# A convolution with max pooling: another load order, another first step, and six column maxima taken in one operation

## The chip, the cores and the metric

The kernel runs on one core of a Trainium2 chip. Its engines work side by side and each takes its own instructions in order: TensorE (PE) multiplies matrices into PSUM, VectorE (DVE) and ScalarE (ACT) work on SBUF and PSUM, GpSimd (POOL) works on SBUF only, and SyncE (SP) issues DMA transfers. An instruction that needs another engine's result waits for it on a semaphore, and everything behind it on the same engine waits too. The metric is the device time of one execution in microseconds (us).

## What is computed

The reference pads each image by one pixel, applies a 3x3 convolution from 64 to 128 channels, and takes the maximum of each 2x2 block. There are 16 images of 64x64.

```python
batch, c_in, h, w, c_out, k = 16, 64, 64, 64, 128, 3
for b, co, ci, kh, kw:   # five loops
    conv[b, co] += weight[co, ci, kh, kw] * x_pad[b, ci, kh:kh+h, kw:kw+w]
output[b, c, i, j] = max(conv[b, c, 2*i:2*i+2, 2*j:2*j+2])
```

## The kernel before

**Tiling.** Two images form a pair: 2 x 64 channels fill 128 partitions, and image l (0 or 1) of a pair uses one half of TensorE's rows. Matmuls of the two halves run at the same time. The 64 rows of an image are cut into four quarters, which gives 8 pairs x 4 quarters = 32 steps. A step makes 8 output rows for each of its two images. SEQ (L10) names the steps: number 0 is K00, 1 is W10, 2 is K01, 3 to 5 are W11, W12 and W13, 6 and 7 are K02 and K03, then the pairs 2 to 7 follow in order. The first digit is the pair, the second the quarter.

**Arithmetic.** Two neighbouring convolution rows have most of their input in common, so the kernel forms sums and differences of input rows and of weights ahead of the products. Each product is three matmuls (kw = 1, 0, 2) of 504 or 512 columns, for one half of one step, and all go through `taps` (L372, matmul at L380). There are two kinds of steps:

- W steps, with four products a half. They need rows prepared: E (difference of even and odd row), S (their sum) and V (differences of rows two apart; for both rows at once, or as two halves Ve and Vo). P2 uses E, P0 and P3 use V, P1 uses S.
- K steps (pair 0), with five products a half. PAa, PAb, PBa and PBb use the input rows as they are, and PR uses KS, a sum of two rows.

Each half step has two PSUM banks, A and B. In a W step P2 goes to A and a copy of A seeds B (SE, ScalarE, L409, once on VectorE as SEv, L407); P0 then adds to A and P3 to B. In a K step PAa and PAb go to A, PBa and PBb to B. In both kinds ScalarE copies A to SBUF (EV, L395 or L397); VectorE takes the row maximum MX of bank B and that copy, back into bank B (L413); and the last product, P1 or PR, adds to B what both rows have in common. That last product therefore waits for MX. Then ScalarE copies the odd columns of B to SBUF (OD, L417), VectorE takes the maximum CM of the even columns and that copy (L423), and a DMA stores the result (ST, L436).

**Weights.** One load (LW) brings all weights. Seven blocks of sums are formed from them as bf16 (`c.` tokens, L215 or L220; GS is an intermediate sum that GM and GP need), turned by TensorE (T, three transposes, L253) and brought to SBUF (TV, L264 or L268). Block D0 serves PBa, D2 PAa, G0 PAb and P0, G2 PBb and P3, G1 PR, GM P2 and GP P1.

**Loads.** Pair 1 (WIDE, L14) stays in fp32 in `wide_x` and is loaded by SP (L278). The first two quarters of pair 0 are loaded as fp32 into `kf` (L283; quarter 0 in the parts a and b) and turned to bf16 in `narrow_x`, odd rows by XO and even rows by XE (L215 or L216). Everything else is loaded by POOL's queue with a cast (LH, L288). The first of these waits for the last XO or XE ahead of it in the order.

**The order.** ORDER (L16) is a list written out, one token for one operation, and the loop at L446 emits the tokens in that order. `MX.5.1` is the row maximum of step 5, half 1; a product's token stands for its next matmul. The letter behind a colon is the engine (v VectorE, a ScalarE, g POOL), a number the PSUM bank. Every engine keeps its own tokens in the order of the list. A row operation on POOL is also held behind the last row operation or cast on VectorE ahead of it in the list (`row_op`, L219).

Of the kernel before, what the change touches and what calls it, by code (L numbers as in the profile page):

```python
# [21 lines left out]
PAa.0.1b PAa.0.0a PAa.0.1b PAa.0.0b PAa.0.1b EV.1.1 PAa.0.0b PAb.0.1b PAa.0.0b PAb.0.1b PAb.0.0a PAb.0.1b
LH.1 PAb.0.0a E.3:v PBa.0.1a:0 TV.G1:a PAb.0.0a PBa.0.0b PBa.0.1a PBa.0.0b PBa.0.1a PBa.0.0b PBa.0.1b EV.0.1
PAb.0.0b PBa.0.1b LH.2 PAb.0.0b PBa.0.1b V.3:v PAb.0.0b P2.3.1:1 PBb.0.0a PBb.0.0a P2.3.1 EV.0.0 PBb.0.0a
LH.3 P2.3.0:4 P2.3.1 P2.3.0 PBb.0.1a PBb.0.1a P2.3.0 SE.3.1:7 PBb.0.1a LH.4 PBb.0.1b KS.0:v PBb.0.0b
PBb.0.1b PBb.0.0b PBb.0.1b PBb.0.0b MX.1.1 P1.1.0 SE.3.0:2 S.3:g P0.3.1 P1.1.0 P0.3.1 P1.1.0 XO.2:a MX.0.0
P0.3.1 P0.3.0 P3.3.1 P0.3.0 P3.3.1 EV.3.1 P0.3.0 MX.0.1 P3.3.1 P3.3.0 P1.1.1 P3.3.0 EV.3.0 E.5:g P1.1.1
P3.3.0 MX.3.1 P1.1.1 PR.0.0 OD.1.0 PR.0.1 PR.0.0 OD.1.1 PR.0.1 MX.3.0 PR.0.0 PR.0.1 XE.2:a PAa.2.0:4 P1.3.1
PAa.2.0 S.5:g CM.1.1 P1.3.1 PAa.2.0 OD.0.1 P1.3.1 P1.3.0 CM.1.0 OD.0.0 PAa.2.1:1 P1.3.0 PAa.2.1 CM.0.1
OD.3.1 P1.3.0 ST.1 PAa.2.1 PAb.2.0 CM.0.0 PAb.2.1 Ve.5:g OD.3.0 PAb.2.0 PAb.2.1 CM.3.1 PAb.2.0 ST.0 PAb.2.1  # L30
PAa.6.0:3 CM.3.0 P2.5.1:0 PAa.6.0 EV.2.1 P2.5.1 KS.6:v PAa.6.0 ST.3 P2.5.1 PAb.6.0 LH.5 PBa.2.1:2 PAb.6.0
KS.2:v PBa.2.1 PAb.6.0 PBa.2.1 PBa.6.0:7 KS.7:v PBb.2.1 EV.6.0 PBa.6.0 PBb.2.1 E.4:v PBa.6.0 PBb.2.1 PBb.6.0
SE.5.1:1 PAa.7.1:5 PBb.6.0 PAa.7.1 MX.2.1 PBb.6.0 Vo.5:g EV.2.0 PAa.7.1 P2.5.0:3 PAb.7.1 P2.5.0 MX.6.0
PAb.7.1 P2.5.0 PAb.7.1 PAa.7.0:4 P0.5.1 SE.5.0:6 PAa.7.0 P0.5.1 LH.6 PAa.7.0 E.9:v P0.5.1 PAb.7.0 EV.7.1
PR.2.1 PAb.7.0 S.8:v PR.2.1 PAb.7.0 EV.5.1 V.9:v PR.2.1 P0.5.0 PBa.7.1:5 P0.5.0 PBa.7.1 EV.7.0 P0.5.0 V.8:v
PBa.7.1 P3.5.0 P3.5.1 EV.5.0 P3.5.0 P3.5.1 P3.5.0 S.9:v P3.5.1 PBa.7.0:0 OD.2.1 P2.9.1:4 E.8:v PBa.7.0
P2.9.1 PBa.7.0 MX.5.1 P2.9.1 V.4:g PBb.7.0 PBb.7.1 PBb.7.0 SE.9.1:3 PBb.7.1 MX.5.0 PBb.7.0 PBb.7.1 PR.6.0
PR.6.0 P0.9.1 PR.6.0 MX.7.0 P0.9.1 P1.5.0 P0.9.1 OD.6.0 P1.5.0 MX.7.1 P1.5.1 P1.5.0 EV.9.1 P1.5.1 PR.7.0
P1.5.1 PR.7.0 S.11:v P3.9.1 PR.7.0 OD.5.0 P3.9.1 P2.9.0:4 CM.6.0 P3.9.1 E.11:g OD.7.0 P2.9.0 CM.5.0 PR.7.1
P2.9.0 OD.5.1 PR.7.1 PBa.2.0:7 CM.7.0 PR.7.1 PBa.2.0 MX.9.1 P2.8.1:6 PBa.2.0 SE.9.0:0 P2.8.1 PBb.2.0 S.4:g  # L40
P2.8.1 PBb.2.0 CM.2.1 OD.7.1 PBb.2.0 P1.9.1 P0.9.0 CM.5.1 P1.9.1 P0.9.0 P1.9.1 CM.7.1 ST.5 P0.9.0 PAa.6.1:1
S.13:g P2.4.0:2 MX.2.0 OD.9.1 PAa.6.1 ST.7 P2.4.0 PAa.6.1 SE.8.1:5 P2.4.0 PAb.6.1 CM.9.1 P3.9.0 PAb.6.1
EV.9.0 P3.9.0 PAb.6.1 Ve.10:v P3.9.0 P0.8.1 SE.4.0:3 PR.2.0 V.13:v P0.8.1 PR.2.0 P0.8.1 PR.2.0 PBa.6.1:4
E.13:v P0.4.0 EV.8.1 PBa.6.1 P0.4.0 PBa.6.1 E.10:v P0.4.0 PBb.6.1 OD.2.0 MX.9.0 P2.8.0:6 PBb.6.1 EV.6.1
V.11:g P2.8.0 PBb.6.1 P2.8.0 P3.8.1 CM.2.0 EV.4.0 P3.8.1 P1.9.0 MX.6.1 P3.8.1 P1.9.0 ST.2 SE.8.0:1 P2.11.1:7
P1.9.0 P2.11.1 P3.4.0 MX.8.1 P2.11.1 OD.9.0 P3.4.0 PR.6.1 P3.4.0 SE.11.1:2 PR.6.1 P0.8.0 CM.9.0 PR.6.1
E.12:g P0.8.0 P1.8.1 MX.4.0 P0.8.0 ST.9 OD.6.1 P1.8.1 P2.13.0:0 P1.8.1 P2.13.0 EV.8.0 CM.6.1 P0.11.1 P2.13.0
P0.11.1 P1.4.0 LH.7 V.12:v OD.8.1 ST.6 P0.11.1 P1.4.0 SE.13.0:6 P2.13.1:4 P1.4.0 P2.13.1 V.14:v P3.8.0
EV.11.1 P2.13.1 P3.8.0 P3.11.1 P3.8.0 CM.8.1 P3.11.1 P0.13.0 OD.4.0 Vo.10:g P3.11.1 P0.13.0 SE.13.1:7 MX.8.0
P2.4.1:5 P0.13.0 P2.4.1 P3.13.0 P2.4.1 EV.13.0 P3.13.0 CM.4.0 P0.13.1 P3.13.0 E.14:v P0.13.1 P1.8.0 SE.4.1:3  # L50
P0.13.1 P1.8.0 MX.13.0 S.10:g P3.13.1 P1.8.0 EV.13.1 P3.13.1 P2.10.0:0 P3.13.1 P2.10.0 MX.11.1 P0.4.1
P2.10.0 OD.8.0 P0.4.1 P1.13.0 P0.4.1 SE.10.0:4 CM.8.0 S.12:g P1.13.0 P1.11.1 P1.13.0 MX.13.1 ST.8 P1.11.1
P2.11.0:1 P1.11.1 OD.13.0 P2.11.0 P3.4.1 P2.11.0 EV.4.1 V.15:v P3.4.1 P0.10.0 P3.4.1 P0.10.0 OD.11.1 P1.13.1
P0.10.0 CM.13.0 SE.11.0:5 P1.13.1 P3.10.0 V.16:g P1.13.1 MX.4.1 P3.10.0 P2.14.1:6 EV.10.0 P3.10.0 P2.14.1
P0.11.0 CM.11.1 P2.14.1 P0.11.0 OD.13.1 P1.4.1 P0.11.0 MX.10.0 SE.14.1:0 P1.4.1 P2.12.0:2 P1.4.1 P2.12.0
CM.13.1 P2.12.0 EV.11.0 P0.14.1 P1.10.0 E.19:v P0.14.1 ST.13 P1.10.0 SE.12.0:7 P0.14.1 P1.10.0 E.18:v
# [469 lines left out]
```

## Time and profile before

| | |
|---|---|
| runs | 101.34, 102.58 and 103.45 us; median 102.58 |
| profiled execution | 101.35 us, span 99.6 us |
| TensorE busy | 93.1 us, 845 matmuls |
| VectorE busy | 91.0 us, 195 operations |
| ScalarE busy | 87.0 us |
| POOL busy | 61.3 us |
| granted TensorE clock | 0.986 on the mean |

The span runs from the first to the last instruction; the execution's own time is 1.75 us longer. Busy time is the time in which at least one instruction of the engine has an open record. Records of neighbouring instructions overlap, since an engine starts one while the end of the one before is still under way, so a row of 0.69 us can stand for 0.60 us of the engine's time. A row of a group ends with the idle time ahead of its instructions and who ended most of it; rows of the timeline begin with start and length in us.

### The profile page before, as it was taken

To read this page: it belongs to the slowest core of one execution; us is meant where nothing else is said; L and a number is where in the kernel's file an instruction comes from. 1 tells how busy PE (TensorE), PEld (TensorE's weight loads), DVE (VectorE), ACT (ScalarE), POOL (GpSimd) and SP (SyncE) were. 2 spreads that over 40 slices of the span, in tenths; PEclk is the share of its full clock that TensorE was granted. 3 is DMA by queue.
4 is the path that set the end of the run, shared out by engine and by line. 5 is a ranking of instruction groups with operands and counts; after the bars stand their busy time and mean duration, and the time that the engine had idled before them with its cause. 6 is when DMAs were issued, how large, how long until landed. Compare 5 with 4: busy or idle time off the path is not lost.

```text
span 99.6 us, 2418 instructions
## 1 busy us (share of the span) xinstructions
PE 93.1 (94%) x845; PEld 61.3 (62%) x845; DVE 91.0 (91%) x195; ACT 87.0 (87%) x196; POOL 61.3 (62%) x58
## 2 busy tenths in 40 slices
...
GB/s 62 286 318 380 336 184 213 213 226 228 246 216 227 226 212 360 230 207 374 148 163 53 109 151 178 205 349 177 16 198 109 105 105 7 100 212 89 73 191 75
DMA packets 11356, 18.81 MB, mean 189 GB/s; under 512 B 848, under 2 KB 9168, under 8 KB 10832
## 3 DMA queue, kind: packets, MB, share of 16 engines
...
q10 hardware_dynamic: 288, 0.20, 0.6%
q8 instruction: 6, 0.10, 0.4%
q14 instruction: 6, 0.05, 0.1%
HBM read 17.07 MB, written 8.39 MB: 256 GB/s over the span
## 4 chain that ended last, share of the span: by engine, by line
PE 87%; DMA 5%; DVE 3%; issue 0%; SPq 0%; DVEq 0%
PE acc L380 86%; DMA wide_x<-in_x_dram 5%; DVE o L423 2%; DVE we L220 1%; PE acc L253 1%; DVE acc L413 0%; SPq L459 0%; DVEq L521 0%
## 5 line engine op out<-in xcount | busy, mean ns | idle before, releaser
L380 PEld LDWEIGHTS <-wt 64*128 64x128 bf16 x816 | 59.0, 94 | 28.9 <-issue 4.0
L380 PE MATMUL acc<-wv,wt 64*128 64x504 bf16 (+1 forms) x240 | 51.8, 377 | 0.0
L380 PE MATMUL acc<-we,wt 64*128 64x512 bf16 (+1 forms) x168 | 42.4, 376 | 0.9 <-DVE we L220 0.9
L413 DVE TENSOR_TENSOR acc<-acc,ev 128x512 f32<-128x512 f32 x64 | 42.4, 689 | 0.7 <-ACT ev L395 0.2
L380 PE MATMUL acc<-ws,wt 64*128 64x512 bf16 (+1 forms) x168 | 40.7, 376 | 0.0
L395 ACT ACTIVATE ev<-acc 128x512 f32<-128x512 f32 x56 | 34.2, 617 | 0.7 <-PE acc L380 0.4
L409 ACT COPY acc<-acc 128x512 f32<-128x512 f32 x55 | 32.9, 601 | 2.0 <-PE acc L380 1.2
L417 ACT COPY od<-acc 128x256 f32<-128x256 f32 x64 | 23.6, 385 | 2.1 <-PE acc L380 1.6
L423 DVE TENSOR_TENSOR o<-acc,od 128x256 f32<-128x256 f32 (+1 forms) x65 | 24.8, 410 | 0.4
L380 PE MATMUL acc<-vh,wt 64*128 64x504 bf16 (+1 forms) x96 | 21.3, 376 | 0.0
L220 POOL TENSOR_TENSOR wv<-narrow_x 128x1024 bf16<-128x1024 bf16 x7 | 14.9, 2130 | 5.3 <-DVE we L220 1.7
L380 PE MATMUL acc<-narrow_x,wt 64*128 64x504 bf16 (+7 forms) x120 | 17.4, 331 | 0.0
L220 POOL TENSOR_TENSOR ws<-narrow_x 128x512 bf16<-128x512 bf16 x12 | 13.7, 1153 | 5.4 <-DVE we L220 2.8
L220 POOL TENSOR_TENSOR we<-narrow_x 128x512 bf16<-128x512 bf16 x9 | 10.3, 1154 | 4.2 <-PE acc L380 1.5
L288 POOL DMA_DIRECT2D narrow_x<-in_x_dram x9 | 5.1, 576 | 8.0 <-ACT narrow_x L215 8.0
L220 POOL TENSOR_TENSOR vh<-narrow_x 128x512 bf16<-128x512 bf16 x5 | 5.8, 1152 | 4.7 <-DVE wv L220 2.1
L220 DVE TENSOR_TENSOR wv<-narrow_x 128x1024 bf16<-128x1024 bf16 x11 | 7.5, 694 | 0.0
L220 DVE TENSOR_TENSOR we<-narrow_x 128x512 bf16<-128x512 bf16 x15 | 6.2, 431 | 0.0
L380 PE MATMUL acc<-ks,wt 64*128 64x504 bf16 (+1 forms) x24 | 5.8, 377 | 0.0
L397 ACT COPY ev<-acc 128x512 f32<-128x512 f32 x8 | 4.8, 596 | 1.0 <-PE acc L380 1.0
L220 DVE TENSOR_TENSOR ws<-narrow_x 128x512 bf16<-128x512 bf16 x12 | 4.9, 412 | 0.0
L441 PE MATMUL acc<-const-bfloat16-1.0 128*128 128x512 bf16 x8 | 3.6, 628 | 0.8 <-PEq L507 0.8
...
## 6 DMA issues: line engine op xcount, KB each, us to landing
out_dram<-o SPq DMA_DIRECT2D x29, 256.0 KB, 3.6
...
narrow_x<-in_x_dram POOLq DMA_DIRECT2D x2, 528.0 KB, 10.3
wide_x<-in_x_dram SPq DMA_DIRECT2D x2, 512.0 KB, 8.6
wide_x<-in_x_dram SPq DMA_DIRECT2D x1, 544.0 KB, 4.9
kf<-in_x_dram SPq DMA_DIRECT2D x1, 512.0 KB, 8.6
...
```

Source lines behind the costliest of these rows:

```text
L220: inst = eng[e].tensor_tensor(out=out, in0=in0, in1=in1, op=op)
L253: nc.tensor.transpose(tp[:, (j - lo) * 128 : (j - lo + 1) * 128], wq[:, BLOCKS[m]].rearrange("a i j c -> a (i j c)")[:, (j - lo) * CI : (j ...
L288: inst = nc.gpsimd.dma_start(out=xs[p][:, lo + 1 : hi + 1, :], in_=rows_of(p, lo, hi))
L380: yield lambda kw=kw, o0=o0, o1=o1, c0=c0, c1=c1: nc.tensor.matmul(acc[t][:, i0:i1, o0:o1], wt[l * CI : l * CI + CI, K * BLOCKS[block] + T ...
L395: nc.scalar.mul(t, acc[bank["A", s, l]], -1.0)
L397: nc.scalar.copy(out=t, in_=acc[bank["A", s, l]])
L409: nc.scalar.copy(out=acc[b], in_=acc[bank["A", s, l]])
L413: nc.vector.tensor_tensor(out=t, in0=t, in1=ev[s, l], op=MAX)
L417: nc.scalar.copy(out=t, in_=acc[bank["B", s, l]][:, :, 1::2])
L423: nc.vector.tensor_tensor(out=ot[s][:, l, i0:i1], in0=acc[bank["B", s, l]][:, i0:i1, 0::2], in1=od[s, l][:, i0:i1], op=MAX,)
L441: nc.tensor.matmul(acc[n], ones[:, 0:128], ones, start=True, stop=True, skip_group_check=True)
```

## The change

Three things change; the products and their number stay.

- The loads of SP come in another order: the weights, then quarter 0 of pair 0 in two parts and quarter 1 (LX.0a, LX.0b, LX.2), and only then the four quarters of pair 1.
- ORDER is another list throughout. The K steps 0 and 2 come first (PBa of step 0 is the first product), then steps 1 and 3. The weight sums D0 and GS are formed by POOL, the casts XE.0b and XO.2 and the turn-out TV.G0 by VectorE, XO.0b by ScalarE. Of the row operations, POOL gets 14 V where it had 8, and 17 E and S where it had 25; VectorE gets 39 E and S where it had 31, 10 V where it had 12, and 2 Ve and Vo where it had 9.
- A token RM takes the column maximum as one VectorE operation from PSUM, in place of an OD and a CM. The list holds six: for half 0 of the steps 22, 24, 28 and 29, and half 1 of the steps 24 and 27. The short description of the change says seven.

```diff
-LW LX.1 LX.0a LX.0b LX.3 LX.2 LX.4 LX.5 c.g0:a c.GS:v c.D2:v c.g2:a T.G0:0 c.GM:v c.g1:a T.G2:1 c.D0:v
-T.GM:2 T.D2:3 E.1:v TV.GM:a TV.D2:a c.GP:v P2.1.0:2 P2.1.1:4 TV.G0:a P2.1.0 P2.1.1 Ve.1:v TV.G2:a P2.1.0
...
+LW LX.0a LX.0b LX.2 LX.1 LX.3 LX.4 LX.5 c.g2:a c.D0:g c.D2:v c.g0:a T.D0:0 c.g1:a XE.0a:v T.D2:1 T.G2:2
+TV.D0:v c.GS:g TV.D2:a T.G0:3 XO.0a:v T.G1:4 XO.0b:a PBa.0.1a:0 PBa.0.0a:5 PBa.0.1a PBa.0.0a XE.0b:v
...
+T.GM:4 XO.2:v XE.2:a T.GP:2 MX.0.0 PAa.2.1:6 PAa.2.0:3 TV.GP:a PAa.2.1 PAa.2.0 PAa.2.1 PAa.2.0 KS.2:v
+TV.GM:a PAb.2.1 PAb.2.0 E.1:v PAb.2.1 PAb.2.0 EV.0.1 PAb.2.1 PAb.2.0 PR.0.0 PBb.0.1b PBb.0.1b LH.0 V.1:v
...
+    def colmax_psum(s, l):
+        nc.vector.tensor_reduce(
+            out=outs(s)[:, l],
+            in_=acc[bank["B", s, l]].rearrange("p h (w c) -> p h w c", c=2),
+            axis=mybir.AxisListType.X,
+            op=MAX,
+        )
...
-            elif name == "OD":
-                odd(s, l)
+            elif name in ("OD", "RM"):
+                {"OD": odd, "RM": colmax_psum}[name](s, l)
```

The diff also lets a load of pair 1, and an E operation, be cut in two; the new list uses neither.

More of the change, by code (lines that the diff above doesn't have):

```diff
@@ L22 @@
[L22 to L56, printed above, removed]
@@ new lines @@
+PBa.0.1b PBa.0.0b PAa.0.1a:1 PBa.0.0b PAa.0.1a PAb.0.0a PAa.0.1a PAb.0.0a PAa.0.1b KS.0:v PAb.0.0a PAa.0.0b
+PAa.0.1b PAa.0.0b PAa.0.1b PAa.0.0b PAb.0.1b c.GP:v PAb.0.0b PAb.0.1b PAb.0.0b PAb.0.1b PAb.0.0b PAb.0.1a
+PBb.0.0b PAb.0.1a PBb.0.0b PAb.0.1a PBb.0.1a EV.0.0 PBb.0.0b PBb.0.1a PBb.0.0a PBb.0.1a PBb.0.0a PBb.0.0a
+T.GM:4 XO.2:v XE.2:a T.GP:2 MX.0.0 PAa.2.1:6 PAa.2.0:3 TV.GP:a PAa.2.1 PAa.2.0 PAa.2.1 PAa.2.0 KS.2:v
+TV.GM:a PAb.2.1 PAb.2.0 E.1:v PAb.2.1 PAb.2.0 EV.0.1 PAb.2.1 PAb.2.0 PR.0.0 PBb.0.1b PBb.0.1b LH.0 V.1:v
@@ new lines @@
+EV.2.1 PR.0.0 PBb.0.1b P2.1.1:1 PR.0.0 P2.1.1 P2.1.0:2 EV.2.0 LH.1 P2.1.1 P2.1.0 PBa.2.1:4 P2.1.0 SE.1.1:6
+PBa.2.1 LH.2 S.1:v PBa.2.0:7 PBa.2.1 PBa.2.0 PBb.2.1 OD.0.0 PBa.2.0 PBb.2.1 E.3:v SE.1.0:3 PBb.2.0 PBb.2.1
+PBb.2.0 P0.1.1 PBb.2.0 MX.0.1 P0.1.1 P0.1.0 V.3:g P0.1.1 P0.1.0 P0.1.0 CM.0.0 EV.1.1 PR.0.1 MX.2.1 PR.0.1
+P2.3.0:5 EV.1.0 PR.0.1 P2.3.0 P2.3.1:1 P2.3.0 MX.2.0 P2.3.1 OD.0.1 P3.1.0 P2.3.1 SE.3.0:2 P3.1.0 PR.2.1
+CM.0.1 P3.1.0 PR.2.1 PR.2.0 E.4:v PR.2.1 LH.3 ST.0 PR.2.0 SE.3.1:0 P3.1.1 PR.2.0 P3.1.1 P0.3.0 S.3:v OD.2.1
@@ new lines @@
+P3.1.1 P0.3.0 P0.3.1 P0.3.0 P0.3.1 CM.2.1 P3.3.0 P0.3.1 V.5:g EV.3.0 P3.3.0 MX.1.0 P3.3.1 P3.3.0 P3.3.1
+EV.3.1 P3.3.1 MX.1.1 PAa.7.0:4 PAa.7.1:5 PAa.7.0 OD.2.0 PAa.7.1 PAa.7.0 PAa.7.1 MX.3.1 P1.1.0 P1.1.1 P1.1.0
+P1.1.1 P1.1.0 P1.1.1 MX.3.0 PAb.7.0 P1.3.1 PAb.7.0 V.4:g OD.1.1 P1.3.1 PAb.7.0 CM.2.0 P1.3.1 OD.1.0 P1.3.0
+PAb.7.1 CM.1.1 P1.3.0 ST.2 OD.3.1 PAb.7.1 P1.3.0 CM.1.0 PAb.7.1 PBa.6.0:6 P2.4.1:7 CM.3.1 OD.3.0 PBa.6.0
+ST.1 P2.4.1 PBa.6.0 EV.7.0 P2.4.1 CM.3.0 P2.4.0:0 PAa.6.1:1 P2.4.0 PAa.6.1 KS.6:v SE.4.1:3 ST.3 P2.4.0
@@ new lines @@
+PAa.6.1 LH.4 PAa.6.0:4 PAb.6.1 EV.7.1 KS.7:v PAa.6.0 PAb.6.1 PAa.6.0 PAb.6.1 LH.5 E.5:v SE.4.0:2 PAb.6.0
+P0.4.1 PAb.6.0 P0.4.1 LH.6 PAb.6.0 V.9:v EV.6.1 P0.4.1 P0.4.0 PBa.7.1:5 P0.4.0 PBa.7.1 EV.6.0 E.9:v P0.4.0
+PBa.7.1 P2.5.0:1 PBb.7.1 E.8:v EV.4.1 P2.5.0 PBb.7.1 P2.5.0 S.5:v PBb.7.1 EV.4.0 P2.5.1:4 PBb.6.0 P2.5.1
+PBb.6.0 MX.7.1 P2.5.1 PBb.6.0 SE.5.0:7 S.4:g P3.4.1 P3.4.0 P3.4.1 P3.4.0 SE.5.1:0 MX.6.0 P3.4.1 P3.4.0
+PR.7.1 P0.5.0 PR.7.1 P0.5.0 MX.4.0 PR.7.1 P0.5.0 V.8:g P0.5.1 P3.5.0 OD.7.1 P0.5.1 P3.5.0 MX.4.1 P0.5.1
@@ new lines @@
+P3.5.0 EV.5.0 P3.5.1 P1.4.0 CM.7.1 P3.5.1 P1.4.0 EV.5.1 P3.5.1 P1.4.0 MX.5.0 P2.8.1:1 PR.6.0 P2.8.1 OD.4.0
+PR.6.0 P2.8.1 PR.6.0 MX.5.1 S.9:g P1.4.1 P1.5.0 P1.4.1 OD.6.0 P1.5.0 CM.4.0 P1.4.1 P1.5.0 P1.5.1 PBa.7.0:4
+CM.6.0 P1.5.1 OD.5.0 PBa.7.0 V.11:v P1.5.1 PBa.7.0 OD.4.1 PBa.6.1:6 PBb.7.0 OD.5.1 PBa.6.1 PBb.7.0 CM.4.1
+PBa.6.1 PBb.7.0 SE.8.1:5 V.10:g P2.9.0:2 PBb.6.1 CM.5.1 ST.4 P2.9.0 PBb.6.1 P2.9.0 CM.5.0 PBb.6.1 P2.8.0:3
+P0.8.1 MX.7.0 SE.9.0:0 ST.5 P2.8.0 P0.8.1 P2.8.0 P0.8.1 P3.8.1 MX.6.1 P0.9.0 SE.8.0:7 P3.8.1 P0.9.0 P3.8.1
@@ L277, in load @@
         if p in WIDE:
-            nc.sync.dma_start(out=xs[p][:, lo + 1 : hi + 1, :], in_=rows_of(p, lo, hi))
+            a, b = {"": (lo, hi), "a": (lo, half(s)), "b": (half(s), hi)}[part]
+            nc.sync.dma_start(out=xs[p][:, a + 1 : b + 1, :], in_=rows_of(p, a, b))
             return
@@ L305, in rows_at, with row_half @@
         return xs[p][:, f : f + 2 * R - 1 : 2, :]
+    def row_half(s, part, e):
+        if part == "a":
+            row["E", s] = row_pool.tile([128, R, W], BF16, name="we")
+        i0, i1 = PARTS[part]
+        row_op(e, row["E", s][:, i0:i1], rows_at(s, 0)[:, i0:i1], rows_at(s, 1)[:, i0:i1], SUB)
     def two_rows(s, name, e):
@@ L417, in odd, with outs, colmax @@
         nc.scalar.copy(out=t, in_=acc[bank["B", s, l]][:, :, 1::2])
-    def colmax(s, l, part):
+    def outs(s):
         if s not in ot:
             ot[s] = o_pool.tile([128, 2, R, WO], FP32, name="o")
+        return ot[s]
+    def colmax_psum(s, l):
[5 more added lines that the diff above has]
+        )
+    def colmax(s, l, part):
         i0, i1 = PARTS[part]
         nc.vector.tensor_tensor(
-            out=ot[s][:, l, i0:i1],
+            out=outs(s)[:, l, i0:i1],
             in0=acc[bank["B", s, l]][:, i0:i1, 0::2],
```

133 lines of the change are left out of this document (72 added, 61 removed).

## The prediction

> **What bounds the kernel now.** I read the page's busy shares first, then the chain that ended last in order of time, then the busy time by stages.
>
> ```profile
> PE 93.1 (94%) x845; PEld 61.3 (62%) x845; DVE 91.0 (91%) x195; ACT 87.0 (87%) x196; POOL 61.3 (62%) x58
> ```
> ```profile
> 1.17 4.89 DMA wide_x<-in_x_dram
> ...
> 6.08 0.70 DVE we L220
> ...
> 6.83 0.82 PE acc L380 x6
> 7.65 0.61 PE acc L253 x9
> 8.26 85.26 PE acc L380 x790
> ```
> ```profile
> 10.00:70.00 60.00, 60.00 (x569) 42.46 (x565) 59.96 (x131) 55.71 (x129) 41.80 (x37) 1.00 0.88 217
> ```
>
> The chain says: pair 1's first load until 6.06, one row difference, then TensorE to the end. But the stage row, whose columns are PE, PEld, DVE, ACT and POOL, then the clock, the DMA share and GB/s, has VectorE busy 59.96 of 60 us too. TensorE's records overlap (each is 0.38 long, and the next of the same half starts after 0.216), so its full row can hide short waits. Here is one, VectorE first, then TensorE:
>
> ```profile
> 52.69 0.41 DVE L220 TENSOR_TENSOR ws<-narrow_x 128x512 bf16<-128x512 bf16 x1
> 53.02 0.41 DVE L220 TENSOR_TENSOR we<-narrow_x 128x512 bf16<-128x512 bf16 x1
> 53.35 0.69 DVE L413 TENSOR_TENSOR acc<-acc,ev 128x512 f32<-128x512 f32 x1
> ```
> ```profile
> 53.40 0.38 PE L380 MATMUL acc<-we,wt 64*128 64x504 bf16 x1
> ...
> 53.62 0.38 PE L380 MATMUL acc<-we,wt 64*128 64x504 bf16 x1
> ...
> 54.09 0.37 PE L380 MATMUL acc<-ws,wt 64*128 64x512 bf16 x1
> ```
>
> The L413 op is MX.12.1; it ends at 54.04, and the product that needs it, P1.12.1, starts 0.05 later, after a hole on its half. So two queues bound this kernel together: TensorE, and VectorE through the row maxima that the last product of each half step waits for.
>
> **Two sums.** For a waiting product I count from the order list the VectorE work up to its maximum and the TensorE work ahead of the product; the difference I call the lead. Costs are starts of neighbours:
>
> ```profile
> 7.82 0.55 DVE L216 CAST narrow_x<-kf 128x256 bf16<-128x256 f32 x2
> ...
> 8.88 0.35 DVE L268 COPY wt<-acc 128x384 bf16<-128x384 bf16 x1
> ...
> 11.15 1.22 DVE L220 TENSOR_TENSOR wv<-wide_x 128x1024 bf16<-128x1024 f32 x1
> ...
> 12.62 3.22 DVE L413 TENSOR_TENSOR acc<-acc,ev 128x512 f32<-128x512 f32 x5
> ...
> 15.75 2.07 DVE L423 TENSOR_TENSOR o<-acc,od 128x256 f32<-128x256 f32 x6
> ...
> 17.21 1.28 POOL L220 TENSOR_TENSOR vh<-wide_x 128x512 bf16<-128x512 f32 x1
> ...
> 17.74 1.72 DVE L220 TENSOR_TENSOR ks<-narrow_x 128x512 bf16<-128x512 bf16 x3
> ...
> 21.95 1.28 DVE L220 TENSOR_TENSOR wv<-narrow_x 128x1024 bf16<-128x1024 bf16 x2
> ```
>
> MX: 0.60 (VectorE's 53.35 row to the next op; five end after 3.22). CM: (2.07-0.41)/5 = 0.33. A bf16 row op of 512: 0.335 (52.69, 53.02, 53.35); of 1024 (V): 0.60. From fp32 0.60 and 1.14 (a record less 0.08 of overlap, as 0.69 gives 0.60). In the same way a cast of 256 costs 0.20, of 320 and a turn-out 0.27, one of 512 by twice the 256 row 0.50, a weight op 0.53, GS 0.42 (their rows are below). A matmul is 0.216 on its half, a quarter-step one half of that, a T 0.17.
>
> *Before*, to MX.12.1: 32 MX 19.2, 29 CM 9.6, 24 bf16 row ops 8.0, 6 V 3.6, from fp32 six 3.6 and one V 1.1, weight ops 2.5, four casts and turn-outs 0.9: 48.7. TensorE: (397 x 0.216 + 48 x 0.109)/2 + 7 x 0.17 = 46.7. Lead 2.07, the largest of the middle. VectorE ended 54.04 - 48.73 = 5.31 behind its own work: 3.80 of start, 0.2 idle, the rest lost, most of it beside POOL (the three KS took 1.72, where they need 1.08: the first ran beside POOL's 17.21 op). TensorE stands at 54.09 - 46.66 = 7.43, and at its last waiting product, P1.27.0 with 86.30 of work ahead, at 8.01: the maximum it needs is the second of this row, which ends at 94.26, so it starts at 94.31. That last number sets the end.
>
> ```profile
> 92.96 1.30 DVE L413 TENSOR_TENSOR acc<-acc,ev 128x512 f32<-128x512 f32 x2
> ```
>
> **The change, part by part.** *The head.* The same loads in another order:
>
> ```profile
> 0.74 0.37 SPq L459 DMA_DIRECT2D wraw<-in_weight_dram  x1
> ...
> 1.17 0.42 SPq L278 DMA_DIRECT2D wide_x<-in_x_dram  x1
> ...
> 1.64 0.90 SPq L283 DMA_DIRECT2D kf<-in_x_dram  x2
> ...
> 3.05 0.43 SPq L283 DMA_DIRECT2D kf<-in_x_dram  x1
> ...
> 3.80 1.75 ACT L215 CAST wq<-wraw 128x256 bf16<-128x256 f32 x3 [1.78 <-DMA wraw<-in_weight_dram]
> 3.80 0.50 DVE L220 TENSOR_TENSOR gsum<-wraw 128x192 f32<-128x192 f32 x1 [3.80 <-DMA wraw<-in_weight_dram]
> 4.22 0.61 DVE L220 TENSOR_TENSOR wq<-wraw 128x256 bf16<-128x256 f32 x1
> ...
> 6.08 0.69 DVE L220 TENSOR_TENSOR we<-wide_x 128x512 bf16<-128x512 f32 x1 [0.19 <-DMA wide_x<-in_x_dram]
> ...
> 10.71 2.82 POOL L288 DMA_DIRECT2D narrow_x<-in_x_dram  x5 [8.01 <-ACT narrow_x L215]
> ```
> ```profile
> wide_x<-in_x_dram SPq DMA_DIRECT2D x1, 544.0 KB, 4.9
> kf<-in_x_dram SPq DMA_DIRECT2D x1, 512.0 KB, 8.6
> ...
> wraw<-in_weight_dram SPq DMA_DIRECT2D x1, 288.0 KB, 3.0
> kf<-in_x_dram SPq DMA_DIRECT2D x1, 288.0 KB, 5.1
> kf<-in_x_dram SPq DMA_DIRECT2D x1, 256.0 KB, 6.9
> ```
>
> Issue plus landing gives bytes by time: 288 KB at 3.7, 832 at 6.1, 1120 at 6.7, 1376 at 9.0 (that issue at 1.64+0.45), 2400 at 11.65. By interpolation LX.0a (576 KB in) lands at 5.0, LX.0b (832) at 6.1, LX.2 (1344) at 8.7, and LX.1, now fifth (1888 KB), at 10.35. Then the first products PBa wait for T.G1, behind the third weight cast (5.55) plus 0.17, and for TV.D0 behind XE.0a: about 5.9 to 6.3, where they started at 6.83. A gain there of 0.5 to 0.9, and 0.6 us of T work (7.65 row) that no longer interrupts. That is not the end's gain: VectorE is now the later one. Its queue up to E.1 holds 4.57 us (D2, GM, GP 1.6; six casts and turn-outs 1.7; two KS 0.67; MX.0.0 0.60), and E.1 waits for LX.1: it starts at 10.38, VectorE 10.38-4.57 = 5.81 behind its work where it was 4.06 before (3.80, the 0.19 of waiting in the 6.08 row, and its overlap). Behind E.1 queue V.1, S.1, E.3 and all maxima; that place costs 1.75 us of VectorE.
>
> D0 and GS go to POOL, for which no row exists: nearest are POOL's 1290 below for 512 and VectorE's 0.61 and 0.50; from these 0.6 to 1.3 each, I take 0.9. With 0.9, D0 is there at 4.7 and the four T ahead of T.G1 fit before 5.6; with 1.3 the first product is 0.2 to 0.4 later, which E.1's wait for LX.1 hides. LH.0 now waits for XE.2 (LX.2 + 0.6, about 9.4) instead of XE.0b (issued 10.71); needed for PAa.7 at about 18, so hidden on both sides.
>
> *Leads.* The five-product steps need few VectorE ops per matmul (no E, S, V), so the largest lead falls. *After* it stands at MX.25.1: 49 MX 29.4, 45 CM 14.9, 34 bf16 row ops 11.4, 8 V 4.8, from fp32 seven 4.2 and one V 1.1, weights 1.6, casts 1.7, one RM 0.6: 69.8; TensorE (600 x 0.216 + 48 x 0.109)/2 + 1.2 = 68.6. Lead 1.25: 0.8 less.
>
> *RM.* Six in the order list (the words say seven), for six OD and six CM:
>
> ```profile
> L417 ACT COPY od<-acc 128x256 f32<-128x256 f32 x64 | 23.6, 385 | 2.1 <-PE acc L380 1.6
> ...
> L220 POOL TENSOR_TENSOR ws<-wide_x 128x512 bf16<-128x512 f32 x3 | 3.9, 1290 | 0.0
> ...
> L220 POOL TENSOR_TENSOR wv<-wide_x 128x1024 bf16<-128x1024 f32 x1 | 2.4, 2360 | 2.1 <-DVE we L220 2.1
> ...
> L407 DVE COPY acc<-acc 128x512 f32<-128x512 f32 x1 | 0.7, 700 | 0.0
> ```
>
> An RM reads 512 fp32 from PSUM as the 0.70 copy does, less overlap 0.60; ends: 0.33 if output counts, 1.14 as the 1024 op. I take 0.60, the nearest row. VectorE as a whole: gone 6 CM 2.0, 2 V 1.2, 5 Ve/Vo 1.7, 2 from fp32 1.2, the seed 0.6, D0 and GS 0.95 = 7.6; new 6 RM 3.6, 5 E/S 1.7, 3 from fp32 1.8, TV.G0 0.3, XO.2 0.5 = 7.9. Even. ScalarE loses some 2.3 us, worth nothing while VectorE is later; if it were not, its cover is gone and TensorE is next. POOL gets six V more (14 for 8); the tightest is V.4: V.5 and V.4, 2.36 each, follow S.3 (VectorE work 11.2, so about 17.0) and are done at 21.7; P0.4.1, with 16.2 of work ahead and TensorE by then at 5.81 + 0.4 of lead + 0.14 = 6.35, wants V.4 at 22.55. 0.85 to spare.
>
> *Sum.* VectorE 5.81 + 0.3 (between 15 and 25 us of TensorE work its lead is only 0.7 to 0.85, so it waits for products) + 0.5 lost beside POOL (bounds 0 and 1.2, what before lost) + 0.09 for the last op's tail = 6.70; + lead 1.25 + 0.05 = TensorE at **8.0**, against 7.43. From there before slipped to 8.01; of that 0.58 I give after 0.4, since at the end its lead is down to 0.15: 8.4, **+0.4 us**. Behind the last product the same OD, two CM halves and stores follow as before, and the 1.75 us around the span stay, so the profiled 101.35 becomes 101.75. That run lies 1.2 below the median; I add 0.45 for where a next run may fall: **102.2**. Measurement here tells 2% from no change, no less.
>
> The trace shows only two-input VectorE ops held by POOL. The Trainium skill, page "SBUF — State Buffer", section "Who interferes with whom", has the fp32 copy hold and be held too. By that rule XO.0a would wait for GS on POOL and the head would be some 0.4 us later, 102.6; the KS row agrees for its kind of op, no row for the copy's.
>
> **Rivals.** *The early start carries (0.25).* LX.1 lands by 10.1, nothing is lost beside POOL and VectorE never waits: 5.53 + 0.09 + 1.25 + 0.05 = 6.9, and with 0.4 of slip 7.3: 0.7 less, 100.65 by the profile. For: the lead does fall by 0.8; against: the interpolated landing. Only were VectorE not binding at all could TensorE's own head (first product at 6.1, 0.84 of T ahead of it, 0.3 of stalls, 0.4 of slip: 6.0, so 2.0 less) give 99.35; I give over 2% a chance of 0.09.
>
> *The reduce is dear (0.13; the slower side).* At two passes (1.14) by MX.31.0 six RM add 3.2. VectorE there is 6.70 + 0.15 + 3.2 = 10.05 against 8.4 without: +1.65, 103.85 with the same allowance. It decides from 1.55/6 = 0.26 more each, that is 0.86. For: no row of it. The Trainium skill, "VectorE: DVE Perf Modes", section "Rules for kernel authors", calls this op the slowest on VectorE; by its table in "The perf-mode tier table", though, it runs at the same 1x, an estimate near 0.70. No run yet shows it.
>
> *POOL is late (0.09).* One V of 2.36 more ahead of V.4, less its 0.85 of cover: +1.5, 103.7.
>
> *The change does not do what it says (0.05).* D0 is so late that products begin at 6.8 again; VectorE still decides, 102.2 to 102.5.
>
> **Chances.** My case 0.48, rivals 0.25, 0.13, 0.09, 0.05. Slower by over 2% takes the dear reduce, half of POOL's case and 0.03 of mine: 0.2. Faster 0.09, within 2% 0.71. The range runs from the early start's 100.65 to the dear reduce's 103.85, a little over for a run's place: 100.6 to 104.0.
>
> **What would show it.** Right: the first L386 product at 5.9 to 6.3; E.1 (fp32 we) at 10.3 to 10.5 released by the wide_x DMA; VectorE without idle from there to 70; P1 products 0.05 behind their maxima in the 60s; RM rows near 0.69. Wrong: P1 well behind its maximum throughout (TensorE alone binds), RM rows over 0.95, or P0 starting with the end of a POOL V.

## The result, and the profile after

| | before | after |
|---|---|---|
| median, 20 runs each on the same chips | 101.9 us (101.04 to 104.65) | 102.85 us (102.18 to 103.95) |
| ratio after to before | | 1.0139, 95% interval 1.011 to 1.0168 |
| profiled execution, span | 101.35 us, 99.6 us | 102.92 us, 101.2 us |
| last L380 or L386 product starts | 94.74 us | 96.08 us |

The changed kernel is slower by 1.4%, within the 2% that I called no change, inside the range, and not at the 102.2 that I gave. The ratios, here and below, leave out executions over 1.5% above the fastest of their kernel, while the medians in us count all: among those left out are six of twelve for less_load (103.6 to 104.3 us, and no profile shows why) and three of six for no_rm, but none of head_free.

Busy shares of the kernel after, from its page:

```profile
PE 94.0 (93%) x845; PEld 57.9 (57%) x845; DVE 91.2 (90%) x193; ACT 86.2 (85%) x189; POOL 65.9 (65%) x57
```

The busy time by stages, of the kernel after (columns PE, PEld, DVE, ACT, POOL, clock, DMA share, GB/s):

```profile
10.00:70.00 60.00, 60.00 (x543) 38.68 (x542) 59.94 (x129) 55.27 (x126) 41.76 (x32) 1.00 0.90 219
70.00:90.00 20.00, 20.00 (x184) 11.80 (x179) 19.85 (x41) 19.20 (x42) 15.56 (x12) 1.00 0.30 102
```

and of the kernel before, for the second stage alone:

```profile
70.00:90.00 20.00, 20.00 (x187) 12.16 (x184) 19.12 (x41) 19.83 (x47) 14.69 (x11) 1.00 0.31 107
```

From 10 to 70 us TensorE and VectorE are both full, as before. From 70 to 90 VectorE is fuller than before (19.85 of 20 against 19.12). This points to the first 11 us: time lost there, which the full queues carry to the end. The experiments test it. The chain that ended last, in order of time, of the kernel after:

```profile
1.17 4.87 DMA kf<-in_x_dram
6.04 0.02 issue
6.06 0.36 DVE narrow_x L215
6.42 0.26 DVE wt L267
6.68 0.79 DVE narrow_x L215
7.46 0.04 issue
7.51 2.38 PE acc L386 x37
9.88 0.44 PE acc L252 x6
10.32 81.26 PE acc L386 x724
```

It has the form of the chain before, a load, an operation on VectorE, then TensorE, but the load is now quarter 0 of pair 0, in its first part LX.0a, and TensorE works without a hole only from 7.51. The start of VectorE's queue shows more (timeline of VectorE, kernel after; start and length in us, and in brackets the idle time ahead):

```profile
3.56 0.61 DVE L219 TENSOR_TENSOR wq<-wraw 128x256 bf16<-128x256 f32 x1 [3.56 <-DMA wraw<-in_weight_dram]
6.06 0.36 DVE L215 CAST narrow_x<-kf 128x320 bf16<-128x320 f32 x1 [1.89 <-DMA kf<-in_x_dram]
6.34 0.34 DVE L267 COPY wt<-acc 128x384 bf16<-128x384 bf16 x1
6.59 1.06 DVE L215 CAST narrow_x<-kf 128x256 bf16<-128x256 f32 x2
...
9.48 0.43 DVE L215 CAST narrow_x<-kf 128x512 bf16<-128x512 f32 x1 [0.16 <-DMA kf<-in_x_dram]
9.99 0.70 DVE L419 TENSOR_TENSOR acc<-acc,ev 128x512 f32<-128x512 f32 x1
10.60 0.41 DVE L219 TENSOR_TENSOR ks<-narrow_x 128x512 bf16<-128x512 bf16 x1
11.08 0.69 DVE L219 TENSOR_TENSOR we<-wide_x 128x512 bf16<-128x512 f32 x1
11.69 1.22 DVE L219 TENSOR_TENSOR wv<-wide_x 128x1024 bf16<-128x1024 f32 x1
12.82 0.69 DVE L219 TENSOR_TENSOR ws<-wide_x 128x512 bf16<-128x512 f32 x1
```

and POOL's two new operations in it, D0 and GS:

```profile
3.61 1.42 POOL L219 TENSOR_TENSOR wq<-wraw 128x256 bf16<-128x256 f32 x1 [0.90 <-DMA wraw<-in_weight_dram]
6.50 0.80 POOL L219 TENSOR_TENSOR gsum<-wraw 128x192 f32<-128x192 f32 x1 [1.48 <-DVE narrow_x L215]
```

The row at 11.08 is E.1, which began at 6.08 before. LX.1, which it reads, landed at 11.05. VectorE would not have reached it much sooner, though: KS.2 starts at 10.60 and takes 0.34 net, so VectorE was free at 10.94. Ahead of KS.2 stand MX.0.0 (9.99), which needs the first products, and XO.2 (9.48), which waited for LX.2 until 9.46. The landings of three loads meet at E.1, and LX.1's came last by 0.1.

### The profile page after: what moved, and what is told of

Read it like the earlier page. It is cut to its first block, busy times and chain, and to the rows that moved or that the text cites. A ratio compares the mean times of both kernels' runs of the same rounds, so it can differ in the third digit from the quotient of the medians.

```text
span 101.2 us, 2407 instructions
## 1 busy us (share of the span) xinstructions
PE 94.0 (93%) x845; PEld 57.9 (57%) x845; DVE 91.2 (90%) x193; ACT 86.2 (85%) x189; POOL 65.9 (65%) x57
## 4 chain that ended last, share of the span: by engine, by line
PE 83%; DMA 5%; DVE 4%; ACT 2%; issue 1%; SPq 0%; DVEq 0%; ACTq 0%
PE acc L386 83%; DMA kf<-in_x_dram 5%; DVE o L440 2%; DVE acc L419 1%; DVE narrow_x L215 1%; ACT ev L401 1%; ACT acc L415 1%; PE acc L252 0%; SPq L476 0%; DVE wt L267 0%; DVEq L540 0%; ACTq L415 0%; DVEq L440 0%
## 5 line engine op out<-in xcount | busy, mean ns | idle before, releaser
L386 PEld LDWEIGHTS <-wt 64*128 64x128 bf16 x816 | 55.7, 94 | 33.8 <-issue 7.6
L386 PE MATMUL acc<-wv,wt 64*128 64x504 bf16 (+1 forms) x288 | 57.3, 376 | 0.0
L386 PE MATMUL acc<-ws,wt 64*128 64x512 bf16 (+1 forms) x168 | 39.5, 376 | 0.0
L386 PE MATMUL acc<-we,wt 64*128 64x512 bf16 (+1 forms) x168 | 39.1, 376 | 0.0
L219 POOL TENSOR_TENSOR wv<-narrow_x 128x1024 bf16<-128x1024 bf16 x11 | 23.4, 2127 | 7.1 <-DVE we L219 2.8
L423 ACT COPY od<-acc 128x256 f32<-128x256 f32 x58 | 21.1, 379 | 3.1 <-PE acc L386 2.9
L440 DVE TENSOR_TENSOR o<-acc,od 128x256 f32<-128x256 f32 (+1 forms) x59 | 22.3, 405 | 0.1
L386 PE MATMUL acc<-narrow_x,wt 64*128 64x504 bf16 (+6 forms) x120 | 15.7, 331 | 0.9 <-DVE wt L267 0.6
L386 PE MATMUL acc<-vh,wt 64*128 64x504 bf16 (+1 forms) x48 | 10.8, 377 | 0.0
L219 POOL TENSOR_TENSOR we<-narrow_x 128x512 bf16<-128x512 bf16 x6 | 6.9, 1155 | 4.9 <-PE acc L386 2.3
L219 POOL TENSOR_TENSOR wv<-wide_x 128x1024 bf16<-128x1024 f32 x3 | 7.0, 2354 | 2.5 <-DVE we L219 1.8
L386 PE MATMUL acc<-ks,wt 64*128 64x504 bf16 (+1 forms) x24 | 6.0, 376 | 0.0
```

Source lines behind the costliest of these rows:

```text
L219: inst = eng[e].tensor_tensor(out=out, in0=in0, in1=in1, op=op)
L386: yield lambda kw=kw, o0=o0, o1=o1, c0=c0, c1=c1: nc.tensor.matmul(acc[t][:, i0:i1, o0:o1], wt[l * CI : l * CI + CI, K * BLOCKS[block] + T ...
L423: nc.scalar.copy(out=t, in_=acc[bank["B", s, l]][:, :, 1::2])
L440: nc.vector.tensor_tensor(out=outs(s)[:, l, i0:i1], in0=acc[bank["B", s, l]][:, i0:i1, 0::2], in1=od[s, l][:, i0:i1], op=MAX,)
```

## The experiments

The texts below name four theories. **V**: VectorE decides, and its place is set by E.1, that is by LX.1's landing. **H**: TensorE's late first product decides, and VectorE only keeps up. **R**: the RM operations are dear. **W**, added after the first runs: TensorE ran slowly in its first 10 us in some executions, and that is the loss. All ratios are to the kernel before, run on the same chip.

### The changed kernel again (after_again)

> The changed kernel once more, as the mark for the runs beside it. Ratio to the kernel before 1.011 to 1.017 as measured. If the late landing of LX.0a (6.06 us) was an accident of one profiled execution, its wait ends nearer 5.0 here; if it belongs to this order of loads, it ends within 0.4 of 6.06 again, and the first product starts near 7.5.

Measured: 103.18 us, ratio 1.0173 (1.0126 to 1.0221). Here LX.0a landed at 4.80, not 6.04, so in the first profile that landing was late by chance; the time is the same. LX.1 landed at 10.61, yet E.1 started at 11.70:

```profile
10.76 0.70 DVE L419 TENSOR_TENSOR acc<-acc,ev 128x512 f32<-128x512 f32 x1 [1.34 <-PE acc L386]
11.37 0.42 DVE L219 TENSOR_TENSOR ks<-narrow_x 128x512 bf16<-128x512 bf16 x1
11.70 0.68 DVE L219 TENSOR_TENSOR we<-wide_x 128x512 bf16<-128x512 f32 x1
```

This time MX.0.0, ahead of E.1 on VectorE, waited 1.34 us for TensorE, whose first transposes ran slowly. This is what theory W is made of; its rows stand in the last section.

### Extra matmuls to keep TensorE busy (after_warm)

```diff
-    for n in range(8):
+    for n in [*range(8), 6, 7]:
...
             turn(args[0], int(at))
+            if args[0] == "G1":
+                for n in (6, 7):
+                    nc.tensor.matmul(acc[n], ones[:, 0:128], ones, start=True, stop=True, skip_group_check=True)
```

> The changed kernel with four more idle-time matmuls on constants: two behind the eight at the start, which then end near 5.2 instead of 4.35, and two between the last T and the first product. Theory W: in most executions of the changed kernel the granted TensorE clock goes to full only at 9 to 10 us (9.07, 9.71 and 10.16 in three profiles, 5.05 and 4.25 in two), since TensorE stands idle from 4.35 to 5.1 and from 5.9 to 6.8; with the idle time filled the clock is full by 7.8 and about 0.6 us of the median goes: ratio to the kernel before 1.006 to 1.012, where the changed kernel had 1.014 and 1.017. Theory V alone (VectorE decides, TensorE's clock in the head is hidden): unchanged, 1.013 to 1.018.

Measured: 102.93 us, ratio 1.0165 (1.0123 to 1.0207). No change. In its profile TensorE was at speed from 5.3 us, and still E.1 started at 11.04 (LX.1 landed at 11.01) and the last product at 96.05, as in the kernel after. The profile of after itself has the transposes at full rate from 5.1 us on and the same loss. W is not the main cause.

### The weight sums back on VectorE (weights_vec)

```diff
-... c.g2:a c.D0:g c.D2:v c.g0:a ...  TV.D0:v c.GS:g TV.D2:a
+... c.g2:a c.D0:v c.D2:v c.GS:v c.g0:a ...  TV.D0:v TV.D2:a
```

> The changed kernel with the weight sums D0 and GS on VectorE again, D0 first, where VectorE stands idle for LX.0a anyway. Takes away POOL's 1.42 us for D0 and the wait of XO.0a beside GS (0.86 instead of 0.28). T.D0 starts near 4.15 instead of 5.1, so the idle gap of TensorE goes too. W: ratio to before 1.004 to 1.011. V: E.1 still waits for MX.0.0 and for LX.1 (10.6 to 11.2), so at most 0.3 us goes: 1.011 to 1.016. If POOL's D0 and the wait beside GS are the whole loss: 0.995 to 1.003.

Measured: 103.06 us, ratio 1.0169 (1.0133 to 1.0205). Timeline of VectorE:

```profile
5.56 0.68 DVE L215 CAST narrow_x<-kf 128x256 bf16<-128x256 f32 x2
...
9.21 0.43 DVE L215 CAST narrow_x<-kf 128x512 bf16<-128x512 f32 x1 [1.31 <-DMA kf<-in_x_dram]
9.55 0.69 DVE L419 TENSOR_TENSOR acc<-acc,ev 128x512 f32<-128x512 f32 x1
10.15 0.42 DVE L219 TENSOR_TENSOR ks<-narrow_x 128x512 bf16<-128x512 bf16 x1
10.92 0.69 DVE L219 TENSOR_TENSOR we<-wide_x 128x512 bf16<-128x512 f32 x1 [0.35 <-DMA wide_x<-in_x_dram]
```

The first product came at 5.70, 1.0 us earlier than in the profile of after, and the two casts that took 1.06 beside POOL took 0.68. Nothing of that is left: XO.2 waits 1.31 for LX.2 (landed 9.19) and E.1 waits 0.35 for LX.1 (landed 10.90). POOL's two operations are not the loss; whatever is gained ahead of these two landings is waited away at them.

### More work on VectorE, ahead of E.1 and behind it (vec_early, vec_late)

vec_early adds two copies of a PSUM bank behind c.D2, where VectorE waits for LX.0a; vec_late adds two fp32 row differences of 512 behind E.1. Neither result is used.

```diff
-... c.D0:g c.D2:v c.g0:a ...
+... c.D0:g c.D2:v ZE c.g0:a ...
+        if name == "ZE":
+            nc.vector.tensor_copy(out=extra, in_=acc[6])
+            nc.vector.tensor_copy(out=extra, in_=acc[7])
```

> The changed kernel with two copies from PSUM on VectorE (0.62 us each, result unused) behind c.D2, where VectorE stands idle for LX.0a from 4.17 to 6.06. V: nothing, ratio to the changed kernel 0.998 to 1.002, because the load is what it waits for. If VectorE's total of work alone counted, whatever its place, it would be 1.011. H: nothing as well, so this run only guards the reading of the late one.

Measured: 103.56 us, 1.0229 (1.018 to 1.0278), 1.0055 times after_again, with intervals that overlap. In its profile E.1 started with the landing of LX.1 again, at 11.55 (landed 11.53): the copies did not push it. The last product came at 96.77, as in after_again, so the profile does not show the 0.5%, which may be the scatter of six runs.

```diff
-... PAb.2.0 E.1:v PAb.2.1 ...
+... PAb.2.0 E.1:v ZL PAb.2.1 ...
+        if name == "ZL":
+            two_rows(1, "E", "v", "spare")
+            two_rows(1, "E", "v", "spare")
```

> The changed kernel with two further fp32 row differences on VectorE (0.60 us each, result unused) right behind E.1. Theory V, VectorE decides from E.1 on: the whole 1.2 us is paid, ratio to the changed kernel about 1.011 (1.008 to 1.014). Rival H, TensorE's late first product decides and VectorE only keeps up: at most a third of it, ratio 1.000 to 1.004. Rival R, only the six reduces near the end cost: 1.000 to 1.004.

Measured: 104.86 us, 1.0333 (1.0282 to 1.0384), 1.0157 times after_again, so +1.7 us for 1.2 us of work. V says this, and H and R do not. In its profile the added row is

```profile
12.65 1.41 DVE L324 TENSOR_TENSOR extra<-wide_x 128x512 bf16<-128x512 f32 x2
```

and E.1 was late too, at 12.04, as in after_again. From E.1 to the last product it took 86.35 us, after_again 85.07: 1.28 us for the 1.2 added.

### More work on TensorE (pe_more)

Three more matmuls a half (P2 of step 1 a first time, 0.65 us) ahead of P2.1.1.

```diff
+                if what == "P2.1.1":
+                    bank["A", 1, 0] = 2
+                    for _ in range(3):
+                        next(taps("P2", 1, 1, ""))()
+                        next(taps("P2", 1, 0, ""))()
```

> The changed kernel with three further matmuls on each half (0.65 us) ahead of P2.1.1, at about 11.5 us. They repeat the first matmul of P2, whose start flag makes the repeat harmless. V: TensorE has that much to spare there, since it comes to be held 2 us later by the maxima of the middle: ratio to the changed kernel 0.999 to 1.003. H: the whole 0.65 is paid, 1.006.

Measured: 104.21 us, 1.0283 (1.0234 to 1.0332), 1.0108 times after_again. From E.1 to the last product 85.72, 0.65 more for 0.65 of work. That is what H says and a miss for V: if VectorE alone decided, TensorE would have hidden it. As vec_late went against H, neither queue decides alone.

### Less work on VectorE (vec_less)

```diff
+        if name == "S" and s in (1, 3):
+            row["S", s] = row["E", s]
+            return
```

> The changed kernel, with S.1 and S.3 (the two fp32 row sums on VectorE for steps 1 and 3) left out: P1 of these two steps reads the E rows in their place, so two steps of the output are not the reference's. VectorE has 1.2 us less to do right behind E.1, TensorE the same. Theory V (VectorE decides from E.1 on): its queue stands 1.2 us earlier from 17 us on, TensorE follows until its own head binds (7.06 us behind its work at 20 us, against 7.9 and more later), so 0.8 to 1.2 us less: ratio to the kernel before 1.003 to 1.007. If VectorE does not decide: 1.014 to 1.017 as the changed kernel. If another queue (ScalarE, POOL) is next in line at once: about 1.010.

Measured: 103.2 us, 1.0174 (1.0118 to 1.0231). No gain, and V falls as I had put it. The timeline of VectorE shows where the 1.2 us went:

```profile
16.49 0.42 DVE L443 TENSOR_TENSOR o<-acc,od 128x256 f32<-128x256 f32 x1 [0.44 <-ACT od L426]
16.83 0.68 DVE L219 TENSOR_TENSOR we<-wide_x 128x512 bf16<-128x512 f32 x1
17.89 0.42 DVE L443 TENSOR_TENSOR o<-acc,od 128x256 f32<-128x256 f32 x1 [0.38 <-ACT od L426]
```

Freed of S.1 and S.3, VectorE waits for OD.0.1, which stands on ScalarE behind EV.1.1 (timeline of ScalarE, the first of the two operations):

```profile
15.11 1.08 ACT L404 ACTIVATE ev<-acc 128x512 f32<-128x512 f32 x2 [0.54 <-PE acc L389]
```

EV.1.1 waited for a product that started at 14.69 and takes 0.38: TensorE is right behind VectorE there. So in this stretch the two queues hold each other with at most some tenths to spare. Work added to either was paid in full, and 1.2 us taken from VectorE alone gave nothing; taking work from TensorE alone was not tried. What is left to try is what both start from.

### A load fewer (less_load), and both starts freed (head_free)

less_load leaves LX.2 out, so the 512 KB ahead of LX.1 in SP's queue are gone, and with them the wait of XO.2. head_free is less_load with D0 and GS on VectorE.

```diff
+        if s == 2:
+            kf[2] = kf[0]
+            return
```

> The changed kernel without the load LX.2 (512 KB, ahead of LX.1 in SP's queue): quarter (0,1)'s casts read quarter (0,0)'s rows, so that quarter of the output is not the reference's. LX.1 lands about 1.3 us earlier, near 9.7. Theory V with LX.1's landing as its start: E.1 starts as soon as VectorE's own queue lets it, 9.9 to 10.8 (its 4.57 us of work ahead, the 0.6 that XO.0a loses beside GS, and LX.0a's landing, which came at 4.8 in one profile and 6.0 in another); the ratio falls to 1.004 to 1.012. If the landing does not matter: E.1 as before or the ratio unchanged, 1.014 to 1.017.

> less_load and weights_vec together: no load LX.2 (the same quarter of the output is wrong), and D0 and GS on VectorE with D0 first, so that POOL holds nothing of VectorE's in the head. VectorE has 0.95 us more to do ahead of E.1, but most of it while it would be idle. Theory V: E.1 at 9.4 to 10.0, where weights_vec alone had 10.92 by LX.1's landing; ratio 1.000 to 1.006, lower than less_load or equal to it. If TensorE's late part alone decides: 1.014 to 1.017.

Measured: less_load 1.0059 (1.0026 to 1.0091), head_free 102.06 us and 1.0049 (1.001 to 1.0088), beside vec_less with 1.0174. The loads by issue, size and median us to landing, less_load first, then the kernel after:

```profile
wide_x<-in_x_dram SPq DMA_DIRECT2D x1, 544.0 KB, 5.7
```
```profile
wide_x<-in_x_dram SPq DMA_DIRECT2D x1, 544.0 KB, 8.5
kf<-in_x_dram SPq DMA_DIRECT2D x1, 512.0 KB, 7.4
```

LX.1 landed at 7.84 (head_free 8.51). E.1 now waits for neither load; timeline of VectorE in less_load:

```profile
8.94 0.70 DVE L422 TENSOR_TENSOR acc<-acc,ev 128x512 f32<-128x512 f32 x1 [0.36 <-PE acc L389]
9.54 0.41 DVE L219 TENSOR_TENSOR ks<-narrow_x 128x512 bf16<-128x512 bf16 x1
9.88 0.68 DVE L219 TENSOR_TENSOR we<-wide_x 128x512 bf16<-128x512 f32 x1
```

E.1 came 1.2 us earlier than in after, the last product 1.1 us earlier (94.97), and the span is 100.3 for 101.2. The next to hold it is TensorE's first step, for whose products MX.0.0 waits 0.36. head_free is the firmer of the two: it differs from weights_vec (1.0169) by the load alone, and the load is worth 1.2%. The 0.5% above the kernel before that is left is not explained. The profiles side by side (us), without no_rm, whose end differs:

| profile | LX.1 landed | E.1 starts | last product | between |
|---|---|---|---|---|
| after | 11.05 | 11.08 | 96.08 | 85.01 |
| after_again | 10.61 | 11.70 | 96.77 | 85.07 |
| after_warm | 11.01 | 11.04 | 96.05 | 85.01 |
| weights_vec | 10.90 | 10.92 | 95.94 | 85.02 |
| vec_early | 11.53 | 11.55 | 96.77 | 85.21 |
| vec_less | 11.46 | 11.48 | 96.31 | 84.83 |
| less_load | 7.84 | 9.88 | 94.97 | 85.10 |
| head_free | 8.51 | 9.71 | 94.79 | 85.08 |
| vec_late, +1.2 on VectorE | 11.24 | 12.04 | 98.39 | 86.35 |
| pe_more, +0.65 on TensorE | 10.90 | 12.29 | 98.02 | 85.72 |

Wherever E.1 starts, between 9.7 and 11.7, the last product follows 84.8 to 85.2 later where no work was added behind E.1. less_load cannot part LX.2's landing, which lets TensorE go on to step 2 and XO.2 run on VectorE, from LX.1's, which lets E.1 go; it removes the wait for both. Of the nine profiles that kept the loads, no_rm's among them, E.1 waited for LX.1 in six, by 0.1 to 0.4 us beyond the end of KS.2; in the other three TensorE's slow start held MX.0.0 and with it E.1. An earlier LX.1 alone would therefore have gained little.

### The RM operations undone, and alone (no_rm, rm_only)

no_rm is the changed kernel with an OD and a CM in place of each RM; rm_only is the kernel before with the same six pairs made RM.

Of the six pairs, the first in no_rm (against the kernel after) and in rm_only (against the kernel before):

```diff
-... P1.22.0 MX.22.1 ... EV.23.1 P2.25.1 RM.22.0 P2.25.0 ...
+... P1.22.0 OD.22.0 MX.22.1 ... EV.23.1 P2.25.1 CM.22.0 P2.25.0 ...
```
```diff
-... P2.25.0 OD.22.0 P0.25.1 ... P3.22.1 CM.22.0 P1.20.0 ...
+... P2.25.0 P0.25.1 ... P3.22.1 RM.22.0 P1.20.0 ...
```

> The changed kernel with each RM taken back into an OD (behind the last P1 of its half step) and a CM. An RM took 0.685 us on VectorE, a CM 0.41, so VectorE has 1.6 us less to do between 72 and 93 us. V: of that only the first counts at the largest lead, 0.2 to 0.5 us less: ratio to before 1.009 to 1.014. Rival R, the reduces are the loss: 1.000 to 1.004. If ScalarE were short (its operations stand in the chain of the end): slower, 1.016 or more.

> The kernel before with only the second part of the change: six of its OD and CM pairs near the end become one VectorE op from PSUM each. Six such ops cost VectorE 0.27 each more than a CM (1.6 us in all) and ScalarE loses 2.3 us. In the changed kernel without them ScalarE was late from 72 us (VectorE idle for od and ev). If the kernel before is short of ScalarE in the same place: 0.2 to 0.6% faster, 0.994 to 0.998. If its VectorE is short there: 1.003 to 1.012. If both have room, as the page's shares from 70 us on (VectorE 9.39 to 9.73 of 10) would let them: 0.999 to 1.002, which I take as likeliest.

Measured: no_rm 105.27 us, 1.0309 (1.0236 to 1.0381); rm_only 102.0 us, 1.0031 (1.0001 to 1.0061). In the new order six RM are worth about 1.7% (1.4% against after_warm and weights_vec, which ran beside no_rm), in the old one they cost 0.3%. Theory R falls. The group of the six in the kernel after, and what VectorE of no_rm waits for from 70 to 92 us (after waits there 0.2 in all):

```profile
L431 DVE TENSOR_REDUCE o<-acc 128x256 f32<-128x512 f32 x6 | 4.1, 679 | 0.2 <-PE acc L386 0.2
```
```profile
DVE o L425 <- ACT od L408: 1.2, 4, 0.5
DVE acc L404 <- ACT ev L386: 0.6, 1, 0.6
```

The new order is short of ScalarE there: with six more copies in its queue, VectorE waits for `od` and `ev`. The two queues keep step to 66 us (as far behind their work as in after) and then fall back, 11.3 us behind at the end for 9.45. No version of the new order beat the kernel before.

### Two casting loads of the kernel before later (casts_later)

```diff
-... EV.0.0 PBb.0.0a LH.3 P2.3.0:4 ... PBb.0.1a LH.4 PBb.0.1b ... Ve.5:g OD.3.0
+... EV.0.0 PBb.0.0a P2.3.0:4 ... PBb.0.1a PBb.0.1b ... Ve.5:g LH.3 LH.4 OD.3.0
```

> The kernel before with two of POOL's load issues (LH.3, LH.4, 0.55 us each) moved behind Ve.5. POOL's row operations of step 5 then end 0.8 us earlier, at 17.7, and the KS operation that lost 0.64 us beside Ve.5 runs at once. The loads are wanted at 35 us and later. V: VectorE gains 0.64 us ahead of the stage where it decides: ratio 0.993 to 0.997. If TensorE alone bound the kernel before: 0.999 to 1.001.

Measured: 101.51 us, 1.0002 (0.9963 to 1.0042). Inconclusive: the row difference on POOL did not move (it started at 17.21 as before), so the collision with KS.6 was still there (KS.6 took 0.77 us, against 1.05 in the profile of before). What the kernel before loses there stays unmeasured.

## Why the prediction was right or wrong

The sum gave 101.75 against a profiled 101.35; the profiled run of after took 102.92. The miss of 1.17 has three parts (they add up to 1.19 by rounding).

- **LX.1's landing was mis-sized: 0.70.** This is the step that failed, and with it the landing of LX.2 ahead of it (9.46 for 8.7). "By interpolation LX.1 at 10.35" went by the bytes of one profile; nine profiles that kept the changed load order gave 10.61 to 11.53, mean 11.07. In the old order the fifth load, LX.3, closes the same 1888 KB and landed at 10.37 in the profile that I used, but at 10.56 and 10.93 in those of rm_only and casts_later: I had the early end of a spread, and the new order is later still. The step behind it, that E.1 then starts with the landing and everything behind it is late by as much, held (11.08), and the table shows the cost is one for one. What I left out is that VectorE's own queue, behind LX.2 and the first products, would have held E.1 nearly as long, until 10.94.
- **From E.1 to the last product: 0.26.** The forecast implies 94.74 + 0.39 - 10.38 = 84.75; it took 85.01. Taking each engine's time at a place less the costs queued ahead of it, VectorE stood at 7.48 behind its work from 66 us (6.70 forecast: 0.70 of landing, 0.08 more), TensorE at 8.80 at P1.25.1, the place of the largest lead (8.0), so the difference of the two, 1.32, was as forecast (1.25 + 0.05): P1.25.1 started 0.06 behind its maximum. The terms that the prediction prints for the two sums add up to 48.5 and 69.7, not 48.7 and 69.8, so by them the leads would be 1.8 and 1.1. To the end TensorE slipped 0.65, not 0.4.
- **The last store: 0.23.** The last CM ends 1.33 later than before, as the last product does, but the execution ends 1.57 later: the last store landed 2.51 after its issue, where it took 2.25 before. I had taken this stretch as unchanged.

The 0.45 for where a next run may fall was right for the kernel before (101.9 against its profiled 101.35); the profiled run of after was already at its median. Adding it to the sum set 102.2 beside the 102.58 of three runs, which made a sum of +0.4 us read like a gain of 0.4%. The kernel became slower, and the interval of the ratio is clear of 1, so the forecast had the direction wrong, while the sum behind it had it right. The ratio was the better frame: 101.75/101.35 is 1.004 where 1.014 was measured. That the range of 100.6 to 104.0 holds the 102.85 shows little, since it was 3.4 us wide.

Step by step, the rest:

- *Two queues bind together.* Right, and more strictly than I used it: vec_late and pe_more are both paid in full. The last product of a half step is released by its maximum as forecast, here MX.19.0 (ends near 66.16) and P1.19.0, in the timelines of VectorE and TensorE of after:

```profile
65.47 1.28 DVE L419 TENSOR_TENSOR acc<-acc,ev 128x512 f32<-128x512 f32 x2
```
```profile
66.21 0.37 PE L386 MATMUL acc<-ws,wt 64*128 64x512 bf16 x1
```

- *First product at 5.9 to 6.3.* 6.74 in the profile of after, where LX.0a landed at 6.04; 6.15 in vec_early and vec_less, 6.11 in less_load. That it is "not the end's gain" was right: weights_vec had it at 5.70 for nothing.
- *D0 and GS at 0.9 each.* 1.42 and 0.80; D0 is above the range of 0.6 to 1.3. "Which E.1's wait for LX.1 hides": right, by weights_vec.
- *RM at the 0.70 copy.* 679 ns, right.
- *V.4 with 0.85 to spare on POOL.* It ended at 22.54 and P0.4.1 started at 23.24: 0.7, no wait.
- *ScalarE's relief is worth nothing.* Wrong. I compared it with a cover that the new order does not have: without the RM, ScalarE is late from 72 us and the kernel is some 1.4 to 1.7% slower.
- *The rival in which the early start carries* fell with the landing, *the dear reduce* with its 679 ns and with rm_only, *POOL late* with V.4; the change did what it says.

The Trainium skill's rule, page "SBUF — State Buffer", section "Who interferes with whom", by which a copy or cast on VectorE can hold POOL and be held by it: the trace agrees. Of the two casts at 6.59, XO.0a ran beside GS and took 0.86; the other took 0.28, and in weights_vec, with no GS on POOL, the two together took 0.68 for 1.06. That it would make the end 0.4 later did not come true: in weights_vec it is gone, and the time is the same. Of the two readings of the page "VectorE: DVE Perf Modes", the one by the section "The perf-mode tier table" was right, 0.68 us; that of "Rules for kernel authors", the slowest op, has no support here, as MX of the same size takes 0.685.
